# A three-pass fp32 decoder on one core: the fifth gate product in 512 columns

## The chip, the core and the metric

The kernel runs on one core of a Trainium2 chip. Its five engines work at the same time, each through its own queue in order: TensorE (PE; its weight loads are PEld), VectorE (DVE), ScalarE (ACT), GpSimd (POOL), and SyncE (SP), which issues DMAs. They wait for each other through semaphores. TensorE writes its results into PSUM banks of 128 x 512 floats; VectorE and ScalarE read them. The metric is the time of one execution in microseconds on the device, as the median of several runs.

## What is computed

A decoder of two layers over 512 tokens of width 1024: a gated short convolution in the first layer, sliding-window attention in the second, and behind each a SwiGLU feed-forward part. The change is in that part:

```python
def swiglu(h, w_gate_up, w_down):
    g, u = jnp.split(h @ w_gate_up, 2, axis=-1)
    return (jax.nn.silu(g) * u) @ w_down
...
    ff = swiglu(rmsnorm(h, ffn_pre_norm[l]), ffn_w_gate_up[l], ffn_w_down[l])
    h = h + rmsnorm(ff, ffn_post_norm[l])
```

`g` and `u` are 2816 wide, in 22 tiles of 128. All is float32.

## The kernel before

**Three passes.** A float32 operand `a` is split into `hi`, its value rounded to TensorE's fast format (`fp32r`), and `lo`, the rest `a - hi`. A product is `hi*lo + hi*hi + lo*hi`. `mm3` (L192 to L195) issues the three matmuls. ScalarE makes `hi` of the weights (L478), VectorE the rest `lo` (L479), on tiles of 128x1024.

**Seven products.** The first two tiles of gate and up are made plainly; the other 20 go in ten groups q0 to q9 per layer (`gate_jobs`). A group is a 2x2 block product, of two halves of the 1024 inputs, two halves of 256 tokens each, and of gate and up, and is computed with seven products instead of eight, from sums of the weight blocks and of the token halves. They run in the order 1, 2, 6, 5, 7, 3, 4. The sums of the token halves are made once per layer. The sums of the weight blocks come by accumulating DMAs that POOL issues (`Sums`, `issue`), for some groups (`ADDED`, q1 and q2 among them) partly by VectorE (L466).

**Banks.** Each product has two output tiles e = 0, 1 (gate and up) of 128 x 256 tokens. `chain` says into which bank a product goes. Products 1, 6, 7, 4 (chain X) accumulate in two banks `gx`, one for each e; in a bank, columns 0 to 255 belong to the rounded tokens and 256 to 511 to their rests: one matmul of 512 columns of `whi` does both (L1072), one of 256 columns of `wlo` with the rounded tokens follows (L1075), and the two column halves are added when they are read. Product 2 (Y, bank `gy`) and products 5 and 3 (Z, one bank `gz` for both e and both products) go through `mm3` in 256 columns. So a product is 16 matmuls in X, and 24 in Y and Z.

**Reading.** After each product `take` reads what has accumulated: `st` is the running sum of X without product 5, `u` the one with it. For products 1, 6 and 4 ScalarE copies the first column half of a bank to `st` and VectorE adds the second (L1050, L1034); for product 7 VectorE adds both halves to `u`. Product 5 alone is in `gz` when ScalarE copies it to `u` (L1039); product 3 is added on top of it in the bank, and VectorE adds the sum to `st` (L1034). A product of X may start only when the bank's state after the product before it has been read.

**Order.** Nothing reorders: each engine's instructions stand as the program issues them. `in_line` runs the products as a line of jobs. Behind job j it prepares the weights of job j + 3 (`LINE_LEAD`; a fetch by SP into one of `N_RAW` = 7 raw tiles, then L478 and L479), so that on VectorE the reading of a product stands ahead of the split for the third product after it. One step of the work left over from the group before (pair sums L593 and L594, splits L599 and L600) is put behind each job. After q2, q4, q6 and q9 come the seven products of the down projection for the groups finished by then (`px`, `py`, `pz`), whose sums VectorE adds up (L648).

Of the kernel before, what the change touches and what calls it, by code (L numbers as in the profile page):

```python
# [12 lines left out]
AF = mybir.ActivationFunctionType  # L13
# [61 lines left out]
def yoco_kernel(  # L75
# [22 lines left out]
    nc = tc.nc  # L98
# [9 lines left out]
    ps_mm = ctx.enter_context(tc.tile_pool(name="ps_mm", bufs=4, space=PSUM))  # L108
    ps_sc = ctx.enter_context(tc.tile_pool(name="ps_sc", bufs=2, space=PSUM))
    ps_pt = ctx.enter_context(tc.tile_pool(name="ps_pt", bufs=2, space=PSUM))  # L110
# [3 lines left out]
    def name(s):  # L114
        uid[0] += 1
        return f"{s}_{uid[0]}"

    def slot(s, dt=F32, w=S):
        return big.tile([P, w], dt, tag="slot", name=name(s), padded_shape=[P, S])

    def wide(s, dt=F32):
        return wides.tile([P, D], dt, tag="wide", name=name(s))
# [7 lines left out]
    def bank(s, pool=None):  # L130

        if pool is None:
            pool = (ps_mm, ps_sc, ps_mm, ps_pt)[turn[0] % 4]
            turn[0] += 1
        return pool.tile([P, S], F32, tag="bank", name=name(s))
# [56 lines left out]
    def mm3(out, whi, wlo, xhi, xlo, start, stop, **kw):  # L192
        nc.tensor.matmul(out, whi, xlo, start=start, stop=False, **kw)  # L193
        nc.tensor.matmul(out, whi, xhi, start=False, stop=False, **kw)  # L194
        nc.tensor.matmul(out, wlo, xhi, start=False, stop=stop, **kw)  # L195
# [256 lines left out]
    class Job:  # L452
# [10 lines left out]
        def add(self):  # L463
            if self.make:
                raw = self.raws[0].tile
                nc.vector.tensor_tensor(out=raw, in0=raw, in1=self.raws[1].tile, op=ALU.add)  # L466
# [90 lines left out]
    for l in range(2):  # L557
# [3 lines left out]
        for rd, (f0, f1) in enumerate(ROUNDS[:-1]):  # L561
            k = slice(f0 // 2, f1 // 2)
# [107 lines left out]
    with tc.manual_schedule(engines=ALL):  # L670
# [25 lines left out]
        for k in range(KT):  # L696
# [7 lines left out]
            for i in range(3):  # L704
                for t in range(3):
# [3 lines left out]
                                     start=k == i == 0, stop=k == KT - 1 and i == 2)  # L709
# [13 lines left out]
        v = small.tile([P, 4], F32, tag="v", name=name("v"))  # L723
# [100 lines left out]
    with tc.manual_schedule(engines=ALL):  # L824
# [21 lines left out]
        pools = {"p": ps_pt, "m": ps_mm, "s": ps_sc}  # L846
# [134 lines left out]
    def ffn(l, before, ahead, gain, gpres, following):  # L981
# [20 lines left out]
        def gate_jobs(q, factors, out, to, then):  # L1002

            sums = sums_of[f"g{l}{q}"]
            a21, a22, a11, a12 = (Raw(b) for b in sums.blocks)
            s1, s3, *rest = (Raw(b) for b in sums.sums)
            raws = {1: [a11], 2: [a12], 5: [s1], 7: [s3], 4: [a22]}
            if rest:  # L1010
                raws[6], raws[3] = ([r] for r in rest)
            else:
                raws[6], raws[3] = [a11, s1], [a12, a11]
            chain = {1: "X", 6: "X", 7: "X", 4: "X", 5: "Z", 3: "Z", 2: "Y"}
            pools = {"X": ps_mm, "Y": ps_pt, "Z": ps_sc}
            split = {}
            if q == 0:

                pools = {"X": ps_sc, "Y": ps_pt, "Z": ps_mm}
                raws[1], raws[2] = [], []  # L1020
                split = {1: ahead.ready[4], 2: ahead.ready[5]}
            banks, kept = {}, []

            def tiles(a):
                return a.rearrange("p (e c) -> p e c", e=2)

            def take(p):
                x, y, z = (banks.get(c) for c in "XYZ")
                st, u, gr = kept
                g0, g1 = (gr.rearrange("p (e h c) -> p e h c", e=2, h=2)[:, :, h]  # L1030
                          for h in range(2))

                def add(out, a, b):
                    nc.vector.tensor_tensor(out=out, in0=a, in1=b, op=ALU.add)  # L1034

                if p == 2:
                    add(g0, tiles(y), tiles(st))
                elif p == 5:
                    nc.scalar.activation(u, z, AF.Copy)  # L1039
                elif p == 3:  # L1040
                    add(g1, tiles(z), tiles(st))
                else:
                    for e in range(2):
                        a, b = x[e][:, :256], x[e][:, 256:]
                        ste, ue = (v[:, e * 256 : (e + 1) * 256] for v in (st, u))
                        if p == 7:
                            add(ue, a, ue)
                            add(ue, b, ue)
                            continue
                        nc.scalar.activation(ste, a, AF.Copy)  # L1050
                        add(ste, b, ste)
                if p == 4:
                    for g, m in ((g0, st), (g1, u)):
                        nc.vector.scalar_tensor_tensor(out=g, in0=tiles(m), scalar=-1.0, in1=g,
                                                       op0=ALU.mult, op1=ALU.mult)

            def run(p):
                def products(job):
                    if not kept:
                        kept.extend([slot("st"), slot("st"), wide("gr")])  # L1060
                    whi, wlo = split[p] if p in split else job.w
                    c = chain[p]
                    opened = c not in banks
                    if opened:
                        banks[c] = ([bank("gx", pools[c]) for _ in range(2)] if c == "X"
                                    else bank("g" + c.lower(), pools[c]))
                    steps = [(e, k, slice(e * S + k * P, e * S + (k + 1) * P))
                             for e in range(2) for k in range(4)]
                    kw = {"skip_group_check": True}
                    if c == "X":  # L1070
                        for e, k, kk in steps:
                            nc.tensor.matmul(banks[c][e], whi[:, kk], factors[p][k][2],  # L1072
                                             start=opened and k == 0, stop=False, **kw)
                        for e, k, kk in steps:
                            nc.tensor.matmul(banks[c][e][:, :256], wlo[:, kk], factors[p][k][0],  # L1075
                                             start=False, stop=k == 3 and p == 4, **kw)
                    else:
                        for e, k, kk in steps:
                            mm3(banks[c][:, e * 256 : (e + 1) * 256], whi[:, kk], wlo[:, kk],
                                *factors[p][k][:2], opened and e == k == 0,  # L1080
                                e == 1 and k == 3 and p in (2, 3), **kw)
                    take(p)
                return products

            def gate():
                nc.scalar.activation(kept[2], kept[2], AF.Silu)  # L1086

            def end():
                late = out(kept[2], to)
                then()  # L1090
                return late

            return [Job(raws[p], run(p), {3: gate, 4: end}.get(p), len(raws[p]) > 1)
                    for p in (1, 2, 6, 5, 7, 3, 4)]
# [42 lines left out]
        with tc.manual_schedule(engines=ALL):  # L1137
# [5 lines left out]
            def then(hf, k):  # L1143
                if hf == 0 and k in (5, 6):
                    for b in ((0, 1), (2, 3))[k - 5]:
                        before.turn(b, (2,))
                if hf == 0 and k == 6:
                    for b in range(4):
                        before.turn(b, (3,))
                    for f in range(KT):  # L1150
                        before.split(0, f, 1)
                    for b in range(4):
                        before.keep(b, 1)
                if hf == 1 and k == 1:
                    factors.update(before.factors())
                if hf == 1 and k == 3:
                    sum_on(f"{l}f0")
# [149 lines left out]
    class Heads:  # L1307
# [115 lines left out]
        def out(self):  # L1423
            if self.t < BOTH:
                hi, lo = halves("ohl", F32R)
            else:
                hi, lo = slot("ohi", F32R), slot("olo", F32R)
            nc.scalar.activation(hi, self.po, AF.Copy)
            nc.vector.tensor_tensor(out=lo, in0=self.po, in1=hi.bitcast(F32), op=ALU.subtract)
            at.append((hi, lo))  # L1430
# [25 lines left out]
    with tc.manual_schedule(engines=ALL):  # L1456
# [20 lines left out]
        for hf in range(2):  # L1477
            c = slice(hf * 256, (hf + 1) * 256)
# [54 lines left out]
    with tc.manual_schedule(engines=ALL):  # L1533
        sum_on("a0")
        for i in range(KT + 2):
# [9 lines left out]
            for c in order.split():  # L1545
# [11 lines left out]
                if op == "g":  # L1557

                    u = 2 * (t - EARLY - 1) + n[0]
# [126 lines left out]
```

## Time and profile before

| | |
|---|---|
| three runs | 1016.07, 1016.13, 1017.07 us, median 1016.13 |
| profiled execution, first to last instruction | 1014.9 us |
| TensorE busy, mean granted clock | 1007.0 us, 0.998 |
| VectorE, ScalarE, GpSimd busy | 867.8, 580.4, 193.8 us |
| gate groups of the first layer | q0 204.6 to 224.4, q1 to 244.2, q2 to 264.1; q3 to q9 between 292.7 and 469.6 |
| gate groups of the second layer | q0 from 702.2, q1 from 722.0, q2 741.8 to 761.7; q3 to q9 between 790.3 and 967.1 |

The profile gives the span of the profiled execution, and no other time of it; the runs were timed on the device from outside, with 1.2 us more. A matmul's row shows its start and a modelled end that overlaps the next one's; so how long a product takes is read from start to start. In a line of the timeline stand the start, the duration of all the merged instructions, the engine, the source line, the operation, out<-in, the shape and the count; in brackets the idle time before it and what ended it.

### The profile page before, as it was taken

How to read it: one execution, taken by the hardware profiler on the slowest of the kernel's cores; microseconds unless marked ns; L12 is line 12 of the kernel's file. 1: busy time of each engine (PE TensorE's matmuls, PEld its weight loads, DVE VectorE, ACT ScalarE, POOL GpSimd, SP SyncE). 2: the span in 40 equal slices, each digit the busy share in tenths (PEclk: the TensorE clock that was granted, in tenths of full speed). 3: DMA queues.
4: the chain of work that ended last, by engine and by line, in shares of the span. 5: the costliest groups of instructions: out<-in, count | busy, mean ns of one | idle time of the engine just before them, and what ended most of it. 6: DMA issues, size and time to landing. Idle time of an engine off the chain costs nothing.

```text
span 1014.9 us, 16253 instructions
## 1 busy us (share of the span) xinstructions
PE 1007.0 (99%) x6008; PEld 893.2 (88%) x6008; DVE 867.8 (86%) x1480; ACT 580.4 (57%) x1035; POOL 193.8 (19%) x259
## 2 busy tenths in 40 slices
PE   9999999999999999999999999999999999999997
PEld 8888888999889898998898888889998998989986
DVE  5766768899788999998878998779997899999896
ACT  6322544875656455566484786677666564645641
POOL 0443133102101011000032753221111010110001
PEclk9999999999999999999999999999999999999999
DMA  9897789549979789779603889976989676979842
GB/s 353 289 246 242 184 253 337 176 166 269 340 238 291 241 285 321 239 212 336 203 2 136 215 241 271 252 276 151 279 282 333 170 248 225 300 263 263 266 155 84
DMA packets 66576, 244.50 MB, mean 241 GB/s; under 512 B 7873, under 2 KB 8385, under 8 KB 54721
## 3 DMA queue, kind: packets, MB, share of 16 engines
q1 hardware_dynamic: 51328, 145.98, 38.8%
q0 software_dynamic: 14592, 96.48, 37.6%
q10 hardware_dynamic: 576, 1.02, 0.3%
q8 instruction: 47, 0.77, 0.3%
q14 instruction: 33, 0.26, 0.1%
HBM read 237.15 MB, written 102.76 MB: 335 GB/s over the span
## 4 chain that ended last, share of the span: by engine, by line
PE 99%; DVE 1%; issue 0%; DVEq 0%
PE gx L1072 15%; PE gx L1075 8%; PE gz L195 4%; PE gz L193 4%; PE gz L194 4%; PE pcub L193 4%; PE pcub L195 4%; PE pcub L194 4%; PE px L193 4%; PE px L194 4%; PE px L195 4%; PE pmix L193 3%; PE pmix L195 3%; PE pmix L194 3%; PE gy L195 2%; PE gy L194 2%
## 5 line engine op out<-in xcount | busy, mean ns | idle before, releaser
L479 DVE TENSOR_TENSOR wlo<-raw,whi 128x1024 fp32r<-128x1024 f32 x225 | 274.6, 1225 | 53.6 <-ACT whi L478 53.4
L478 ACT ACTIVATE whi<-raw 128x1024 fp32r<-128x1024 f32 x225 | 233.6, 1051 | 100.7 <-DVE raw L466 28.9
L1072 PE MATMUL gx<-xt,whi 128*128 128x512 f32 x480 | 120.4, 393 | 0.0
L1072 PEld LDWEIGHTS gx<-xt,whi 128*128 128x128 f32 x480 | 86.3, 189 | 15.5
L547 POOL DMA_DIRECT2D hsum<-in_w_gb_dram x96 | 62.8, 733 | 150.6 <-ACT whi L478 90.1
L547 POOL DMA_DIRECT2D hsum<-hsum x32 | 25.3, 790 | 295.5 <-ACT whi L478 198.2
L1034 DVE TENSOR_TENSOR st<-gx,st 128x256 f32<-128x256 f32 x200 | 78.0, 419 | 2.5 <-ACT st L1050 0.4
L1050 ACT ACTIVATE st<-gx 128x256 f32<-128x256 f32 x120 | 43.4, 380 | 62.6 <-PE gx L1075 58.9
L1075 PEld LDWEIGHTS gx<-xt,wlo 128*128 128x128 f32 x480 | 65.5, 190 | 4.7
L1075 PE MATMUL gx<-xt,wlo 128*128 128x256 f32 x480 | 66.9, 282 | 0.0
L1086 ACT ACTIVATE gr<-gr 128x1024 f32<-128x1024 f32 x20 | 21.2, 1062 | 49.9 <-DVE gr L1034 49.9
L193 PE MATMUL px<-wlo,ahi 128*128 128x512 f32 x120 | 46.7, 389 | 0.0
L194 PE MATMUL px<-whi,ahi 128*128 128x512 f32 x120 | 46.7, 389 | 0.0
L195 PE MATMUL px<-whi,alo 128*128 128x512 f32 x120 | 46.7, 389 | 0.0
L195 PE MATMUL gz<-xhi,wlo 128*128 128x256 f32 x160 | 45.5, 284 | 0.0
L193 PE MATMUL gy<-xlo,whi 128*128 128x256 f32 x160 | 45.3, 283 | 0.0
L194 PE MATMUL gy<-xhi,whi 128*128 128x256 f32 x160 | 45.3, 283 | 0.0
L195 PE MATMUL gy<-xhi,wlo 128*128 128x256 f32 x160 | 45.3, 283 | 0.0
L193 PE MATMUL gz<-xt,whi 128*128 128x256 f32 x160 | 45.3, 283 | 0.0
L194 PE MATMUL gz<-xt,whi 128*128 128x256 f32 x160 | 45.3, 283 | 0.0
L195 PE MATMUL gz<-xt,wlo 128*128 128x256 f32 x160 | 45.3, 283 | 0.0
L193 PE MATMUL gz<-xlo,whi 128*128 128x256 f32 x160 | 45.3, 283 | 0.0
(298 smaller groups left out, 2989.0 us busy)
## 6 DMA issues: line engine op xcount, KB each, us to landing
hsum<-in_w_gb_dram POOLq DMA_DIRECT2D x96, 512.0 KB, 7.8
raw<-hsum SPq DMA_DIRECT2D x88, 512.0 KB, 8.0
raw<-in_w_gb_dram SPq DMA_DIRECT2D x60, 512.0 KB, 7.0
hsum<-in_w_dn_dram POOLq DMA_DIRECT2D x36, 512.0 KB, 8.0
raw<-in_w_dn_dram SPq DMA_DIRECT2D x32, 512.0 KB, 6.3
hsum<-hsum POOLq DMA_DIRECT2D x28, 512.0 KB, 5.6
raw<-in_w_in_dram SPq DMA_DIRECT2D x21, 512.0 KB, 7.4
hsum<-in_w_dn_dram POOLq DMA_DIRECT2D x12, 768.0 KB, 12.9
```

The source lines that it names most:

```text
L193: nc.tensor.matmul(out, whi, xlo, start=start, stop=False, **kw)
L194: nc.tensor.matmul(out, whi, xhi, start=False, stop=False, **kw)
L195: nc.tensor.matmul(out, wlo, xhi, start=False, stop=stop, **kw)
L478: self.begun = nc.scalar.activation(hi[:, :n], raw, AF.Copy)
L479: nc.vector.tensor_tensor(out=lo[:, :n], in0=raw, in1=hi[:, :n].bitcast(F32), op=ALU.subtract)
L547: nc.gpsimd.dma_start(dst, src, max_dma_last_dim=4 * 4 * S, **kw))
L1034: nc.vector.tensor_tensor(out=out, in0=a, in1=b, op=ALU.add)
L1050: nc.scalar.activation(ste, a, AF.Copy)
L1072: nc.tensor.matmul(banks[c][e], whi[:, kk], factors[p][k][2], start=opened and k == 0, stop=False, **kw)
L1075: nc.tensor.matmul(banks[c][e][:, :256], wlo[:, kk], factors[p][k][0], start=False, stop=k == 3 and p == 4, **kw)
L1086: nc.scalar.activation(kept[2], kept[2], AF.Silu)
```

## The change

Product 5 takes the wide form of X: two banks (`gz`, one for each e), `whi` with 512 columns of rounded tokens and rests, `wlo` with 256 columns. Product 3 gets a bank of its own, `gv`, from the pool of product 2 (`ps_pt`), and stays in 256 columns. Since product 5 is no longer in product 3's bank, VectorE adds it to `st`; and since its two column halves are apart, ScalarE copies the first of each e to `u`, and VectorE adds the second.

```diff
-            chain = {1: "X", 6: "X", 7: "X", 4: "X", 5: "Z", 3: "Z", 2: "Y"}
-            pools = {"X": ps_mm, "Y": ps_pt, "Z": ps_sc}
+            chain = {1: "X", 6: "X", 7: "X", 4: "X", 5: "Z", 3: "V", 2: "Y"}
+            pools = {"X": ps_mm, "Y": ps_pt, "V": ps_pt, "Z": ps_sc}
             split = {}
             if q == 0:
 
-                pools = {"X": ps_sc, "Y": ps_pt, "Z": ps_mm}
+                pools = {"X": ps_sc, "Y": ps_pt, "V": ps_pt, "Z": ps_mm}
...
                 elif p == 5:
-                    nc.scalar.activation(u, z, AF.Copy)
+                    for e in range(2):
+                        ue = u[:, e * 256 : (e + 1) * 256]
+                        nc.scalar.activation(ue, z[e][:, :256], AF.Copy)
+                        add(ue, z[e][:, 256:], ue)
+                    add(st, u, st)
                 elif p == 3:
-                    add(g1, tiles(z), tiles(st))
+                    add(g1, tiles(v), tiles(st))
...
                     if opened:
-                        banks[c] = ([bank("gx", pools[c]) for _ in range(2)] if c == "X"
-                                    else bank("g" + c.lower(), pools[c]))
+                        banks[c] = ([bank("g" + c.lower(), pools[c]) for _ in range(2)]
+                                    if c in "XZ" else bank("g" + c.lower(), pools[c]))
...
-                    if c == "X":
+                    if c in "XZ":
                         for e, k, kk in steps:
                             nc.tensor.matmul(banks[c][e], whi[:, kk], factors[p][k][2],
                                              start=opened and k == 0, stop=False, **kw)
                         for e, k, kk in steps:
                             nc.tensor.matmul(banks[c][e][:, :256], wlo[:, kk], factors[p][k][0],
-                                             start=False, stop=k == 3 and p == 4, **kw)
+                                             start=False, stop=k == 3 and p in (4, 5), **kw)
```

VectorE in q1 of the first layer, from the sums of product 6 to those of product 7 (the number behind a name tells tiles apart; `raw`, `whi`, `wlo` are weights, `s`, `gr`, `ahi`, `alo` the left-over work of the group before). Before:

```order
L1034 TENSOR_TENSOR st_2238<-gx_2242,st_2238 128x256
L479 TENSOR_TENSOR wlo_2326<-raw_1994,whi_2325 128x1024
L593 TENSOR_TENSOR s_2236<-gr_2014 128x256
L594 SCALAR_TENSOR_TENSOR s_2236<-s_2235,gr_2014 128x256
L479 TENSOR_TENSOR wlo_2367<-raw_2076,whi_2366 128x1024
L600 TENSOR_TENSOR alo_2374<-s_2235,ahi_2373 128x512
L1034 TENSOR_TENSOR st_2239<-gx_2241,st_2239 128x256 x2
L1034 TENSOR_TENSOR st_2239<-gx_2242,st_2239 128x256 x2
```

The same place now:

```order
L1034 TENSOR_TENSOR st_2236<-gx_2240,st_2236 128x256
L479 TENSOR_TENSOR wlo_2324<-raw_1994,whi_2323 128x1024
L593 TENSOR_TENSOR s_2234<-gr_2014 128x256
L594 SCALAR_TENSOR_TENSOR s_2234<-s_2233,gr_2014 128x256
L1034 TENSOR_TENSOR st_2237<-gz_2338,st_2237 128x256
L1034 TENSOR_TENSOR st_2237<-gz_2339,st_2237 128x256
L1034 TENSOR_TENSOR st_2236<-st_2237,st_2236 128x512
L479 TENSOR_TENSOR wlo_2362<-raw_2076,whi_2361 128x1024
L600 TENSOR_TENSOR alo_2369<-s_2233,ahi_2368 128x512
L1034 TENSOR_TENSOR st_2237<-gx_2239,st_2237 128x256 x2
L1034 TENSOR_TENSOR st_2237<-gx_2240,st_2237 128x256 x2
```

Three adds stand between the pair sums and the next weight's rest; all else keeps its order.

ScalarE at the same place, around product 5. Before:

```order
L478 ACTIVATE whi_2325<-raw_1994 128x1024
L1039 ACTIVATE st_2239<-gz_2340 128x512
L478 ACTIVATE whi_2366<-raw_2076 128x1024
L599 ACTIVATE ahi_2373<-s_2235 128x512
L478 ACTIVATE whi_2397<-raw_2105 128x1024
```

The same place now:

```order
L478 ACTIVATE whi_2323<-raw_1994 128x1024
L1041 ACTIVATE st_2237<-gz_2338 128x256
L1041 ACTIVATE st_2237<-gz_2339 128x256
L478 ACTIVATE whi_2361<-raw_2076 128x1024
L599 ACTIVATE ahi_2368<-s_2233 128x512
L478 ACTIVATE whi_2392<-raw_2105 128x1024
```

One copy has become two of half the width; nothing else has moved.

More of the change, by code (lines that the diff above doesn't have):

```diff
@@ L1027, in take @@
             def take(p):
-                x, y, z = (banks.get(c) for c in "XYZ")
+                x, y, z, v = (banks.get(c) for c in "XYZV")
                 st, u, gr = kept
```

## The prediction

> **What bounds the kernel now.** I read the page first: its busy times, the granted clock and the chain that ended last.
>
> ```profile
> PE 1007.0 (99%) x6008; PEld 893.2 (88%) x6008; DVE 867.8 (86%) x1480; ACT 580.4 (57%) x1035; POOL 193.8 (19%) x259
> ...
> PEclk9999999999999999999999999999999999999999
> ...
> PE 99%; DVE 1%; issue 0%; DVEq 0%
> ```
>
> TensorE runs through almost without a gap at full clock and is 99% of the chain, so time taken out of its stream should come out of the total. But VectorE is at 86%, and that is a mean. So the second view was the busy time per stage: each row below is one gate group (seven products, q0, q1, q2, q5 of the first layer, then q1 and q2 of the second).
>
> ```profile
> core 0: us, PE busy (x) PEld busy (x) DVE busy (x) ACT busy (x) POOL busy (x), PEclk, DMA share, GB/s
> 204.61:224.42 19.81, 19.81 (x137) 18.47 (x137) 17.84 (x30) 14.24 (x22) 1.82 (x3) 1.00 0.63 213
> 224.42:244.25 19.83, 19.83 (x137) 18.47 (x137) 19.69 (x32) 12.37 (x20) 4.45 (x7) 1.00 0.72 202
> 244.25:264.15 19.90, 19.90 (x137) 18.52 (x137) 19.77 (x32) 12.38 (x20) 3.67 (x6) 1.00 1.01 328
> ...
> 351.24:371.03 19.79, 19.79 (x137) 18.47 (x136) 18.04 (x28) 11.65 (x17) 2.81 (x5) 1.00 0.71 252
> ```
>
> ```profile
> 721.98:741.79 19.81, 19.81 (x137) 18.47 (x137) 19.67 (x32) 12.35 (x19) 3.65 (x6) 1.00 0.89 295
> 741.79:761.70 19.91, 19.91 (x138) 18.52 (x137) 19.77 (x32) 12.38 (x20) 2.38 (x3) 1.00 0.85 245
> ```
>
> In q1 and q2 of either layer VectorE is busy 19.7 of 19.8 to 19.9 us: two engines are full there. In q5, as in the groups not shown, it has 1.3 to 3.4 us to spare. The chain of waits in order of time says the same: the eight wide matmuls of product 7, 1.84 us in nearly every group, take 0.1 us more in q2 of both layers.
>
> ```profile
> 255.59 1.94 PE gx L1072 x8
> ...
> 753.13 1.95 PE gx L1072 x8
> ```
>
> **The change, part by part.** *TensorE gains.* The timeline of TensorE in q5: product 6 (wide form), product 5 (old form, 24 matmuls of 256 columns), product 7 (wide form), and the start of product 3.
>
> ```profile
> 356.89 2.00 PE L1072 MATMUL gx<-xt,whi 128*128 128x512 f32 x8
> ...
> 359.68 0.28 PE L193 MATMUL gz<-xt,whi 128*128 128x256 f32 x1
> ...
> 362.56 2.00 PE L1072 MATMUL gx<-xt,whi 128*128 128x512 f32 x8
> ...
> 365.36 0.28 PE L193 MATMUL gz<-xlo,whi 128*128 128x256 f32 x1
> ```
>
> From start to start, the old form takes 362.56 - 359.68 = 2.88 us, the wide one 2.79 (359.68 - 356.89) and 2.80. The columns are the same, 6144; only eight starts fewer remain as a gain. Product 5 becomes 0.085 us shorter, 20 times: 1.7 us, which on a full TensorE all counts.
>
> The Trainium skill, TensorE: Matmul & The Clock Gate, section Back-to-back issue gap, puts the gap of matmuls at N/2.4 + 2.5 ns, which would make product 5 shorter by eight times 2.5 = 20 ns and the whole gain 0.4 us. The rows above say 0.085 us a product, and the measurement decides; by the page the sum below would be 0.9 us higher (0.065 less gain in seven groups of each layer).
>
> *ScalarE* copies product 5's first column half in two pieces of 128x256 instead of one of 128x512. The first bank is complete four matmuls before the second, so the first piece goes earlier. ScalarE is busy 12 to 14 of 19.8 us: nothing.
>
> *Banks.* Product 3 opens a bank in the pool of product 2; the two alternate, each read long before its next turn. Product 5's two banks are free again after VectorE's adds, one group ahead of their next use. Nothing, unless VectorE is a whole product behind.
>
> *VectorE* gets three adds behind product 5: two of 128x256 from the banks, one of 128x512 in SBUF. Nothing is taken from it. Its rows in q1 give the prices, and show the place: product 6's sums (235.03), a weight rest, two pair sums, then (at 237.50) the rest and the split before which the three adds now stand, and product 7's sums (239.23).
>
> ```profile
> 235.03 0.75 DVE L1034 TENSOR_TENSOR st<-gx,st 128x256 f32<-128x256 f32 x2
> 235.69 1.22 DVE L479 TENSOR_TENSOR wlo<-raw,whi 128x1024 fp32r<-128x1024 f32 x1
> ...
> 237.16 0.42 DVE L594 SCALAR_TENSOR_TENSOR s<-s,gr 128x256 f32<-128x256 f32 x1
> 237.50 1.22 DVE L479 TENSOR_TENSOR wlo<-raw,whi 128x1024 fp32r<-128x1024 f32 x1
> 238.63 0.69 DVE L600 TENSOR_TENSOR alo<-s,ahi 128x512 fp32r<-128x512 f32 x1
> 239.23 1.67 DVE L1034 TENSOR_TENSOR st<-gx,st 128x256 f32<-128x256 f32 x4
> ```
>
> ```profile
> 239.68 0.42 DVE L1034 TENSOR_TENSOR st<-gx,st 128x256 f32<-128x256 f32 x1
> ```
>
> What counts is from start to start, since instructions overlap a little. Two independent adds take 235.69 - 235.03 = 0.66, so 0.33 each. An add that needs the one before it starts 239.68 - 239.23 = 0.45 later. A 128x512 takes 239.23 - 238.63 = 0.60. So: first add 0.33, second 0.45 (the third reads its result), third 0.60: 1.38 us. Bounds: 0.33 + 0.33 + 0.60 = 1.26 if nothing waits, 0.42 + 0.42 + 0.69 = 1.53 if nothing overlaps. I take 1.38, as each of the three has its like in these rows.
>
> *Where the adds are hidden.* In q0, q5 and q6 VectorE sits idle at exactly this place, waiting for the next weight's rounding by ScalarE, which queues behind the copy of product 5:
>
> ```profile
> 216.01 0.42 DVE L594 SCALAR_TENSOR_TENSOR s<-s,gr 128x256 f32<-128x256 f32 x1
> 217.57 1.22 DVE L479 TENSOR_TENSOR wlo<-raw,whi 128x1024 fp32r<-128x1024 f32 x1 [1.14 <-ACT whi L478]
> ```
>
> ```profile
> 215.99 0.60 ACT L1039 ACTIVATE st<-gz 128x512 f32<-128x512 f32 x1 [1.55 <-PE gz L195]
> ```
>
> ```profile
> 364.34 1.23 DVE L479 TENSOR_TENSOR wlo<-raw,whi 128x1024 fp32r<-128x1024 f32 x1 [1.03 <-ACT whi L478]
> ...
> 384.15 1.22 DVE L479 TENSOR_TENSOR wlo<-raw,whi 128x1024 fp32r<-128x1024 f32 x1 [1.20 <-ACT whi L478]
> ```
>
> In q0 the adds can follow the pair sums at 216.35 (216.01 plus 0.34, as from 237.16 to 237.50) and end at 217.73, while the rest started at 217.57: 0.16 us late. The second bank's copy must end by 216.7 for that: it can begin where the old copy of both did, at 215.99, and take no longer, so it ends by 216.6. So q0 leaves a lag of 0.16, with 0 to 0.4 as bounds. The groups behind q2 have the same idle place, like q5 and q6 here; the 0.2 to 0.4 us that stick out of it meet the rest of their spare time (q5: 18.04 busy of 19.79). Eight groups of a layer pay nothing.
>
> *Where it is not.* From 217.57 until 270.3 VectorE has no gap beyond 0.04 us. A lag can't be made up there: it is 0.16 until product 5 of q1, 1.54 until product 5 of q2, 2.92 after it. TensorE feels it because products 6, 7 and 4 add into the banks that VectorE must have read after the product before: the next may start when the second half of the first bank is read. The three closest places, VectorE's last read and TensorE's start behind it (q2, before products 6, 7 and 4):
>
> ```profile
> 249.15 0.42 DVE L1034 TENSOR_TENSOR st<-gx,st 128x256 f32<-128x256 f32 x1
> ```
>
> ```profile
> 249.76 1.32 PE L1072 MATMUL gx<-xt,whi 128*128 128x512 f32 x5
> ```
>
> ```profile
> 254.95 0.42 DVE L1034 TENSOR_TENSOR st<-gx,st 128x256 f32<-128x256 f32 x1
> ```
>
> ```profile
> 255.43 0.73 PE L1072 MATMUL gx<-xt,whi 128*128 128x512 f32 x2
> ```
>
> ```profile
> 259.61 0.42 DVE L1034 TENSOR_TENSOR st<-gx,st 128x256 f32<-128x256 f32 x1
> ```
>
> ```profile
> 261.20 2.00 PE L1072 MATMUL gx<-xt,whi 128*128 128x512 f32 x8
> ```
>
> The middle pair is the wait already there: read until 255.37, start at 255.43, so the handover costs 0.06. With the lags: product 6 can start at 249.57 + 1.54 + 0.06 = 251.17 instead of 249.76 (1.41 late), product 7 at 255.37 + 1.54 + 0.06 = 256.97 (1.54 late), product 4 at 260.03 + 2.92 + 0.06 = 263.01 instead of 261.20 (1.81 late). These are not added: each is TensorE's delay so far, with its gain in q0 to q2 within it. Most of it falls in front of product 6 of q2.
>
> *What is late next.* After q2 come the down products, each of which needs its weight's rest. The tightest is the third:
>
> ```profile
> 266.80 3.49 DVE L479 TENSOR_TENSOR wlo<-raw,whi 128x1024 fp32r<-128x1024 f32 x3
> 273.96 3.50 DVE L479 TENSOR_TENSOR wlo<-raw,whi 128x1024 fp32r<-128x1024 f32 x3 [3.67 <-ACT whi L478]
> ```
>
> ```profile
> 269.46 0.39 PE L193 MATMUL px<-wlo,a 128*128 128x512 f32 x1
> ```
>
> It is ready at 266.80 + 1.22 = 268.02, with the lag at 270.94; it is wanted at 269.46 + 1.81 = 271.27. It holds by 0.33 us. Then 3.67 us of idle time take up VectorE's lag. The DMA issues of SP and POOL, paced by these splits, move by no more than that lag.
>
> *Sum.* A layer: +1.81 at the end of q2, minus 7 x 0.085 = 0.6 in q3 to q9: +1.21. The second layer has the same rows: +1.21. Together +2.4 us on a span of 1014.9. The median of the runs, 1016.13, lies 1.2 us above that span: 1016.1 + 2.4 = 1018.5. By the bounds (adds 1.26 to 1.53, q0's lag 0 to 0.4), a layer gives +0.8 to +1.75, and the time is 1017.7 to 1019.6.
>
> **Rivals.** *VectorE's adds are hidden everywhere, TensorE's gain alone remains*: 1016.1 - 1.7 = 1014.4, not slower. The place is product 4 of q2: TensorE starts 1.17 us after the read, less 0.06, so a lag under 1.11 costs nothing there; it decides whether three adds, paid twice, come to less than 0.5 us each time. For it speaks TensorE's 99%; against it the rows of 19.7 us. The Trainium skill, Perfetto Trace Analysis, section Identifying the Most-Contended Engine, calls the engine of highest occupancy the one to optimise first, which would be TensorE and this time; the same section grants that the engine can change over time, which the rows of q1 and q2 show. Chance 0.11.
>
> *The lag is paid once, not twice*: VectorE gains it back between product 5 of q1 and that of q2, as some of its waits shrink while TensorE stands. Then a layer costs 0.16 + 1.38 - 1.11 - 0.6 = -0.2, in all 1015.8. Against it: no gap is in those rows. Chance 0.15.
>
> *The lag spreads*: the down rests, held by 0.33 us, or weight tiles freed up to 2.9 us later, come too late; the DMA share of 1.01 in q2 leaves no room to catch up. Another 1 to 3 us a layer: 1020.5 to 1024.5. Chance 0.12.
>
> **How the numbers follow.** The forecast has 0.62, with 1017.7 to 1019.6 as its own range. A measurement tells about 0.2%, 2.0 us, from no change, so slower begins at 1018.2; the forecast reaches it unless the adds cost 1.28 or less: 0.50 of its 0.62 lie above. With the spreading lag, slower is 0.62. Same: 0.12 of the forecast, 0.15 of the lag paid once, 0.07 of the hidden adds, 0.34. Faster keeps 0.04, if the gain of 1.7 us is a little larger than it looks. The range 1015.6 to 1020.2 leaves out the hidden adds and most of the spreading lag, 0.2 together.
>
> **What would show it.** Product 5 from start to start 2.79 to 2.80 us. Behind it, three VectorE instructions at starts 0.33, 0.45 and 0.60 apart; in q0 and q5 VectorE's idle time there all but gone. In q1 and q2 VectorE without a gap for 21 us a group; product 6 of q2 about 1 us late in the chain of waits, product 4 of q2 about 1.8 us later than before, in both layers, and every other group 0.085 shorter. I am wrong if VectorE finds room in q1 or q2, if the adds cost less than 1.28, or if a down product of the first round waits for its weight.

## The result and the profile after

The changed kernel takes 1019.1 us (median of eight runs, 1018.79 to 1019.86) against 1016.42 before (eight runs, 1016.03 to 1017.07): a ratio of 1.0027, with a 95% interval of 1.0017 to 1.0037. It is 2.7 us slower. The profiled execution has a span of 1017.0 us (1014.9 before).

The page of the changed kernel: busy times, then the shares of the chain that ended last.

```profile
PE 1006.7 (99%) x5848; PEld 884.2 (87%) x5848; DVE 893.3 (88%) x1540; ACT 582.8 (57%) x1055; POOL 195.2 (19%) x259
...
PE 89%; DVE 8%; issue 2%; DMA 0%; DVEq 0%; SPq 0%; ACT 0%; ACTq 0%
```

TensorE issues 160 matmuls fewer, and VectorE is busy 25.5 us longer (867.8 to 893.3). The mean shares of the span hardly move. The chain does: VectorE held 1% of it, now 8%. That the end hangs on VectorE somewhere is read there, not in the 88%.

What TensorE's wide matmuls waited for, in the view of waits (us in total, times, longest us):

```profile
PE gx L1076 <- DVE st L1034: 2.2, 6, 0.7
```

Six waits in the whole run, three a layer (shorter ones are not listed). The busy times by stage say where: q0, q1, q2 of the first layer, then q1 and q2 of the second, in the columns of the same view of before.

```profile
203.62:223.35 19.73, 19.73 (x130) 18.05 (x129) 18.86 (x32) 14.17 (x23) 1.83 (x3) 1.00 0.63 213
223.35:243.88 20.53, 20.33 (x131) 18.21 (x129) 20.36 (x34) 11.74 (x20) 4.47 (x7) 1.00 0.72 205
243.88:264.90 21.02, 20.16 (x128) 17.92 (x127) 20.85 (x35) 12.32 (x20) 3.68 (x6) 1.00 0.95 316
...
722.38:742.89 20.51, 20.31 (x130) 18.22 (x129) 20.34 (x34) 11.74 (x20) 3.65 (x6) 1.00 0.85 287
742.89:764.20 21.31, 20.41 (x130) 18.18 (x129) 21.14 (x35) 12.34 (x20) 2.38 (x3) 1.00 0.85 250
```

Each row is length, then busy us by engine. q0 is 0.08 us shorter than before. q1 has grown by 0.7 us in either layer, and q2 of the second layer by 1.4. The row of q2 of the first layer ends 0.29 us before the group does (the first down product starts at 265.19), so q2 is 21.31 us long there and has grown by 1.4 too. VectorE is busy in all but 0.2 us of each row of q1 and q2: here it sets the pace, and TensorE now has idle time (20.16 busy of 21.02).

The timeline of TensorE in q5, from product 5 (now on `gz` in wide form) over product 7 to product 3:

```profile
360.71 2.00 PE L1076 MATMUL gz<-xt,whi 128*128 128x512 f32 x8
...
363.50 2.00 PE L1076 MATMUL gx<-xt,whi 128*128 128x512 f32 x8
366.30 0.28 PE L193 MATMUL gv<-xlo,whi 128*128 128x256 f32 x1
```

Product 5 takes 363.50 - 360.71 = 2.79 us from start to start (2.88 before), product 7 2.80 as before. The gain of the change is there, 0.09 us a product.

The timeline of VectorE in q0, from the second pair sum over the three adds (the first two in one row) to the next weight's rest:

```profile
215.20 0.42 DVE L594 SCALAR_TENSOR_TENSOR s<-s,gr 128x256 f32<-128x256 f32 x1
215.54 0.75 DVE L1034 TENSOR_TENSOR st<-gz,st 128x256 f32<-128x256 f32 x2
216.32 0.69 DVE L1034 TENSOR_TENSOR st<-st,st 128x512 f32<-128x512 f32 x1
216.93 1.22 DVE L479 TENSOR_TENSOR wlo<-raw,whi 128x1024 fp32r<-128x1024 f32 x1
```

The adds take 216.93 - 215.54 = 1.39 us. The bracket of idle time (1.14 us) in front of the rest is gone. In q1 the same rows stand at 236.85, 237.63 and 238.24: 1.39 again, with no idle time there to be used up.

Last, the places at which TensorE paid in q2: VectorE's read for which product 6 waits, and the start of product 6.

```profile
249.90 0.42 DVE L1034 TENSOR_TENSOR st<-gx,st 128x256 f32<-128x256 f32 x1
```

```profile
250.37 0.50 PE L1076 MATMUL gx<-xt,whi 128*128 128x512 f32 x1 [0.66 <-DVE st L1034]
```

And the same before product 4, where the read stood 1.2 us clear of TensorE before:

```profile
261.74 0.42 DVE L1034 TENSOR_TENSOR st<-gx,st 128x256 f32<-128x256 f32 x1
```

```profile
262.31 2.09 PE L1076 MATMUL gx<-xt,whi 128*128 128x512 f32 x8 [0.20 <-DVE st L1034]
```

From 217 us, the weight's rest in q0, until the second of these places the chain of waits of the changed kernel never comes to TensorE; it follows VectorE from instruction to instruction, and enters TensorE with product 4 of q2 (part of it):

```profile
248.84 1.14 DVE wlo L479
249.98 0.67 DVE st L1034 x2
...
261.74 0.44 DVE st L1034
262.18 0.14 issue
262.31 2.09 PE gx L1076 x8
```

**Where the 2.7 us came from.** The starts of TensorE's products can be taken from both traces and subtracted, product by product. From q0's start to the first down product, the changed kernel loses 2.02 us in either layer. Each product 5 in q3 to q9 then gives 0.09 back; in q9 product 6 costs 0.15 (it starts 0.04 late and takes 0.11 longer), and product 3 gives 0.11 back. In all 0.57 comes back a layer. So a layer costs 1.45 us, 2.9 in all. The spans differ by only 2.1, because in this execution the first matmuls of the program, far from the change, ran 0.8 us sooner; the medians, 2.7 apart, don't rest on one execution.

### The profile page after: what moved, and what is told of

Its sections match the earlier page's. It is cut to its first block, busy times and chain, and to the rows that moved or that the text cites. A ratio compares the mean times of both kernels' runs of the same rounds, so it can differ in the third digit from the quotient of the medians.

```text
span 1017.0 us, 16055 instructions
## 1 busy us (share of the span) xinstructions
PE 1006.7 (99%) x5848; PEld 884.2 (87%) x5848; DVE 893.3 (88%) x1540; ACT 582.8 (57%) x1055; POOL 195.2 (19%) x259
## 4 chain that ended last, share of the span: by engine, by line
PE 89%; DVE 8%; issue 2%; DMA 0%; DVEq 0%; SPq 0%; ACT 0%; ACTq 0%
PE gx L1076 12%; PE gx L1079 6%; PE pcub L194 4%; PE pcub L195 4%; PE pcub L193 4%; PE px L194 4%; PE px L193 4%; PE px L195 4%; PE gz L1076 3%; PE pmix L194 3%; PE pmix L193 3%; PE pmix L195 3%; DVE wlo L479 2%; PE pz L195 2%; PE pz L194 2%
## 5 line engine op out<-in xcount | busy, mean ns | idle before, releaser
L195 PE MATMUL gv<-xhi,wlo 128*128 128x256 f32 x160 | 45.3, 283 | 0.0
L193 PE MATMUL gv<-xlo,whi 128*128 128x256 f32 x160 | 45.3, 283 | 0.0
L194 PE MATMUL gv<-xhi,whi 128*128 128x256 f32 x160 | 45.2, 283 | 0.0
L547 POOL DMA_DIRECT2D hsum<-in_w_dn_dram x48 | 31.7, 754 | 46.5 <-ACT whi L478 31.3
L1076 PE MATMUL gz<-xt,whi 128*128 128x512 f32 x160 | 40.1, 392 | 0.0
```

Source lines behind the costliest of these rows:

```text
L547: nc.gpsimd.dma_start(dst, src, max_dma_last_dim=4 * 4 * S, **kw))
```

## The experiments

My theory, A: product 5's gain of 0.085 us is real in every group; the cost is VectorE's three adds, and only where VectorE has no idle time, in q1 and q2 of each layer. Each experiment was timed against the kernel before, run in turn on the same chip; its median there lay between 1016.5 and 1016.7. Differences below are between medians; the intervals are those of the ratio.

### Which groups pay

Two complements. The first keeps the old form in q1 and q2 alone, the second has the new form only there. Rival B says that the cost is spread over all groups.

```diff
+            apart = q not in (1, 2)      # second kernel: apart = q in (1, 2)
-            chain = {1: "X", 6: "X", 7: "X", 4: "X", 5: "Z", 3: "V", 2: "Y"}
+            chain = {1: "X", 6: "X", 7: "X", 4: "X", 5: "Z", 3: "V" if apart else "Z", 2: "Y"}
...
+                elif p == 5 and not apart:
+                    nc.scalar.activation(u, z, AF.Copy)
...
-                    add(g1, tiles(v), tiles(st))
+                    add(g1, tiles(v if apart else z), tiles(st))
...
-                    if c in "XZ":
+                    if c in ("XZ" if apart else "X"):
```

> The changed kernel with the old form of products 5 and 3 in q1 and q2 of both layers, the new one in the other sixteen groups. Theory A (VectorE is full in q1 and q2 alone, the adds cost only there, each group gains 0.085 us on TensorE): q0's lag of about 0.2 us still meets the tight places of q1 and q2 (+0.2 a layer), the seven groups behind gain 0.6, q9 gives 0.15 back: -0.3 a layer, about 0.6 us less than before. Theory B (adds or banks cost something in every group, 2.7 us over 20 groups): 16 of 20 shares, +2.1 us.

> The new form in q1 and q2 of both layers alone. Theory A: VectorE's lag 1.38 behind product 5 of q1, 2.76 behind that of q2; less the 1.17 of room in front of product 4 of q2, plus 0.1 to 0.2 for handover and restart: +1.7 to +1.8 a layer, about +3.5 us in all, more than the whole change costs. Theory B (a share in every group): 4 of 20, +0.5 us.

Without q1 and q2: 1015.66 us, 0.9 faster than before (0.998 to 0.9997). With them alone: 1020.38, 3.8 slower (1.0021 to 1.0045). The two add up to 2.9, near the change's cost (2.7 by the medians, 2.9 by the trace). In the trace of the second, each layer loses 1.84 us in q0 to q2, as A has it; B, which had +2.1 and +0.5, falls.

Sixteen products at 0.085 us would be 1.36; A took q0's lag off and had 0.6. From the start of its first gate group to the end of its last one the trace gains 0.76. It shows what is missing: 0.23 to 0.25 us a layer in q1, from q0's lag, and some 0.05 net in q9, as in the change.

### The two halves of the change apart

The adds alone: the kernel before, with three adds of the same shapes and kinds of operands put behind product 5's copy (what they write is overwritten later). And the new form alone: the changed kernel without the adds.

```diff
 # the adds alone, against the kernel before
                     nc.scalar.activation(u, z, AF.Copy)
+                    for e in range(2):
+                        c = slice(e * 256, (e + 1) * 256)
+                        add(gr[:, e * 512 + 256 : e * 512 + 512], y[:, c], u[:, c])
+                    add(g1, tiles(u), g1)
```

```diff
 # the new form alone, against the changed kernel
                         nc.scalar.activation(ue, z[e][:, :256], AF.Copy)
-                        add(ue, z[e][:, 256:], ue)
-                    add(st, u, st)
```

> The kernel before, with three VectorE adds of the same shapes behind product 5 that write a place overwritten later; the products and banks are the old ones. Theory A (VectorE's time is the whole cost): as the change without its gain on TensorE, and with 0.25 more lag from q0, where the old copy of both halves ends later: +2.2 to +2.5 a layer, +4.4 to +5.0 us. Theory C (the banks cost: product 3 in the pool of product 2, product 5 in both banks of its pool): no change, within 0.5 us of before.

> The changed kernel without the three VectorE adds behind product 5 (so the rests' half of product 5, and product 5 in the second sum, are left out of the result); products and banks are the new ones. Theory A: TensorE's gain alone, 20 x 0.085 = 1.7 us less than before, and up to 0.2 more where q2 waited 0.1 us. Theory C (the banks cost): +2.7 us, as with the whole change. Theory B: in between.

The new form alone: 1014.53 us, 2.06 faster (0.9968 to 0.9987). Its trace has no wait for VectorE on TensorE. This is the gain, at last undisturbed: 0.09 us off in each of the 20 groups, 1.7 in all, and 0.1 more in q9 of each layer, in product 3 (the next kernel shows why). The expectation looked for such an addition in q2; there it is 0.03.

The adds alone: 1022.55 us, 6.0 slower (1.0043 to 1.0068), a full microsecond above what A expected. The trace gives 2.3 us a layer in q1 and q2, as expected, and 0.86 a layer in q9, which A had as a group that pays nothing: 0.41 in product 6, by the lag that q8 hands on (the change has 0.15 there), and 0.45 in product 3. Theory C (the banks cost) falls with both kernels: the new banks alone cost nothing, the adds alone cost more than the change. For product 3, VectorE in q9, before:

```profile
462.63 1.22 DVE L479 TENSOR_TENSOR wlo<-raw,whi 128x1024 fp32r<-128x1024 f32 x1 [2.23 <-ACT whi L478]
```

And TensorE there, at the first matmul of product 3 that uses this rest:

```profile
463.91 0.39 PE L195 MATMUL gz<-xhi,wlo 128*128 128x256 f32 x1
464.13 0.28 PE L193 MATMUL gz<-xlo,whi 128*128 128x256 f32 x1
```

With the adds alone:

```profile
463.83 0.76 DVE L1034 TENSOR_TENSOR gr<-gy,st 128x256 f32<-128x256 f32 x2 [1.28 <-ACT st L1039]
464.62 0.69 DVE L1034 TENSOR_TENSOR gr<-st,gr 128x512 f32<-128x512 f32 x1
465.23 1.22 DVE L479 TENSOR_TENSOR wlo<-raw,whi 128x1024 fp32r<-128x1024 f32 x1
```

And TensorE there, in product 3:

```profile
465.91 0.28 PE L194 MATMUL gz<-xhi,whi 128*128 128x256 f32 x1
466.50 0.38 PE L195 MATMUL gz<-xhi,wlo 128*128 128x256 f32 x1 [0.31 <-DVE wlo L479]
```

VectorE had 2.23 us of idle time there, more than the adds need, but in this kernel it spends 1.28 of it waiting for ScalarE's copy of both halves, and the adds come behind that wait. The weight's rest behind them is wanted by product 3. In the kernel before it ended at 462.63 + 1.22 = 463.85, and TensorE used it at 463.91, 0.06 us later; the next matmul started 0.22 us behind, where 0.12 is usual. So there was no room at all. Idle time in front of an instruction is no cover if its result is wanted at once. In the changed kernel and in the new form alone ScalarE copies in two pieces and gets to this weight sooner; the wait does not appear, and the 0.1 us come back.

### How much of the adds must go

The changed kernel without the third add.

```diff
-                    add(st, u, st)
```

> The changed kernel without the third of the three adds (128x512); product 5 is left out of the second sum. Theory A (VectorE's lag in q1 and q2): two adds are 0.67 us a group. q0 hides them; behind product 5 of q1 the lag is 0.67, and products 6 and 7 of q2 had 0.13 and 0 us of room: +0.67 a layer at the end of q2. Behind q2's product 5 it is 1.34, within 0.3 us of what product 4 had, so nothing more. Then -0.6 in the seven groups behind, and q9 waits no more. Between -0.2 and +0.5 us against before, so between no adds (-2.1) and three (+2.7), not on the straight line between them (+1.1). Rival: the cost is proportional to the adds' time, +0.2 to +0.3 is a straight line through the origin at half the price; then q2's product 4 starts 0.9 us late a layer.

1015.6 us, 0.9 faster (0.9982 to 1.0: the interval touches no change): a miss of my expectation, which had it between -0.2 and +0.5. With no adds the time is 2.1 below before, with two 0.9 below, with three 2.7 above. So the first two cost 1.1 us and the third 3.6: not a price per add, but a delay that is free up to a point. What the expectation lacked is that q0 passes on not a lag of 0 but a lead of 0.3 us: with the copy in two pieces ScalarE gets to the next weight's rounding sooner, and VectorE to its rest (12.82 us after q0's start, 13.12 before). Two adds take 0.66 us in q2 (257.05 to 257.71); paid twice and less the lead, that is 1.0, and product 4 of q2 has 1.11 us of room. TensorE waits once in each layer, before product 6 of q2:

```profile
PE gx L1075 <- DVE st L1034: 0.5, 2, 0.3
```

### Less work for VectorE in q1 and q2

The weight sums that VectorE makes in q1 and q2 (L466) are left out in the first kernel, and made by accumulating DMAs, as in most other groups, in the second.

```diff
 # left out
-                raws[6], raws[3] = [a11, s1], [a12, a11]
+                raws[6], raws[3] = ([a11], [a12]) if q in (1, 2) else ([a11, s1], [a12, a11])
```

```diff
 # made by DMAs
-ADDED = (1, 2, 3, 4, 5, 7)
+ADDED = (3, 4, 5, 7)
```

> The changed kernel with VectorE's two sums of weight blocks left out in q1 and q2 (products 6 and 3 there use one block instead of a sum, so the result is another). Theory A: VectorE has 2 x 1.14 us more room in each of these groups, the three adds (1.4 us) fit in, and TensorE's gain remains: 1.4 to 1.9 us less than before. Rival (the three adds hold TensorE up by where they stand, not by VectorE's fullness): +2 us or more, as with the change.

> The changed kernel with all weight sums of q1 and q2 made by accumulating DMAs, as in q0, q6, q8 and q9, instead of two of them by VectorE. Theory A: VectorE gets the room as if they were left out, 1.4 to 1.9 us less than before, as long as the DMAs come in time. Rival E (the DMA engines are full there too, their share was 1.01 in q2 of the first layer): the weights come late, and it is slower than before by more than 1 us.

Left out: 1014.82 us, 1.9 faster (0.9978 to 0.9995; its runs scatter from 1014.1 to 1017.6). The profiled execution came 1.9 us late to q0 and had made that up by the end. With all three adds in place, TensorE waits nowhere in q1 and q2, and they are 0.1 and 0.2 us shorter than before; what was short there was VectorE's time, and not the place of the adds, as the rival had it.

Made by DMAs: 1030.74 us, 14 slower (1.0124 to 1.0152). A's gain had as its condition that the DMAs come in time; the rival, that they don't, is right, and by far more than it said. Busy time by stage, q2 of that kernel:

```profile
247.30:267.00 19.70, 19.70 (x129) 18.04 (x128) 18.17 (x32) 10.13 (x18) 3.66 (x6) 1.00 1.03 359
```

Its chain of waits, from q2 on (two long steps of many):

```profile
247.49 19.85 DMA raw<-hsum
...
273.52 15.73 DMA raw<-hsum
```

q2 is 19.70 us, not 21.31, and VectorE has 1.5 us to spare: the cure works where it is applied, and q1 and q2 gain as much as with the sums left out. But the DMA share in q2 is 1.03 (1.01 in the kernel before, 0.95 in the changed one), and a fetch of a summed block, in q2 and again behind it, is 16 to 20 us of the chain. The weights behind q2 come late, and TensorE loses 3.2 us in the first down round. It loses 8.6 more between the layers. There it waits for ScalarE's normalised tokens (4.0 us at once); the chain leads from them to GpSimd, whose own small steps of that normalisation stand in its queue behind the DMAs of the weight sums, 12 to 14 us each on the chain. The kernel also came 3.2 us late to q0; there it prepares the weights of the convolution in another order too, and that part is not explained here. In q2 there is nothing left on the DMAs to give.

### The adds on GpSimd

GpSimd is busy 19%. First the third add goes there; then all three (ScalarE copying both column halves).

```diff
-                    add(st, u, st)
+                    nc.gpsimd.tensor_tensor(out=st, in0=u, in1=st, op=ALU.add)
```

```diff
-                        add(ue, z[e][:, 256:], ue)
-                    add(st, u, st)
+                        ve = gr[:, e * S + 256 : (e + 1) * S]
+                        nc.scalar.activation(ve, z[e][:, 256:], AF.Copy)
+                        nc.gpsimd.tensor_tensor(out=ue, in0=ue, in1=ve, op=ALU.add)
+                    nc.gpsimd.tensor_tensor(out=st, in0=u, in1=st, op=ALU.add)
```

> The changed kernel with the third add behind product 5 (128x512, SBUF alone) on GpSimd instead of VectorE. Theory A (VectorE's lag): two adds are 0.67 us a group; q0 hides them, the lag is 0.67 behind product 5 of q1 and meets q2's products 6 and 7, which had 0.13 and 0 us of room: +0.7 a layer, then -0.6 by TensorE's gain: between 0 and +0.5 us against the kernel before, so about 2.3 us less than the whole change. Rival D (GpSimd's add of 1.3 us hinders VectorE or comes too late for product 3's sum): no better than the change, +2.7 us.

> The changed kernel with nothing of product 5 on VectorE: ScalarE copies both column halves, GpSimd adds them and adds the sum to the other one (128x512 about 1.3 us by its rows). Theory A: as with the adds left out, 1.5 to 2.0 us less than before, if GpSimd ends about 3 us behind product 5, when VectorE wants the sum for product 7. Rival D: GpSimd waits for the paced DMAs in its queue, or ScalarE's two more copies delay the weights: slower than before by 1 us or more.

One add moved: 1024.95 us, 8.3 slower (1.0071 to 1.0098). Three moved: 1034.33, 17.7 slower (1.0161 to 1.0189). Rival D, in the expectations, had the direction; neither loss was foreseen at that size. GpSimd's add in q0 and in q1, third add moved:

```profile
216.80 1.29 POOL L1043 TENSOR_TENSOR st<-st,st 128x512 f32<-128x512 f32 x1 [1.93 <-DVE st L1034]
...
238.71 2.21 POOL L1043 TENSOR_TENSOR st<-st,st 128x512 f32<-128x512 f32 x1 [2.09 <-DVE st L1034]
```

VectorE at the second of them:

```profile
238.54 1.21 DVE L479 TENSOR_TENSOR wlo<-raw,whi 128x1024 fp32r<-128x1024 f32 x1
239.68 1.79 DVE L600 TENSOR_TENSOR alo<-s,ahi 128x512 fp32r<-128x512 f32 x1
241.39 0.87 DVE L1034 TENSOR_TENSOR st<-gx,st 128x256 f32<-128x256 f32 x2
```

Read the three instructions by their ends. VectorE's rest runs from 238.54 at its usual 1.21 us. GpSimd's add starts at 238.71, inside it, and takes 2.21 instead of 1.29, until 240.92. VectorE's split takes 1.79 instead of 0.69, from 239.68 on: 1.1 us of standing still on the engine that has no time. In q0 it is the other way round: GpSimd starts first, at 216.80, and takes its 1.29; VectorE's rest, from 216.88, takes 2.30 instead of 1.22. The groups of that kernel say that it is no single case (mean ns behind the comma):

```profile
L600 DVE TENSOR_TENSOR alo<-s,ahi 128x512 fp32r<-128x512 f32 x40 | 38.4, 960 | 0.1
...
L1043 POOL TENSOR_TENSOR st<-st,st 128x512 f32<-128x512 f32 x20 | 36.0, 1802 | 55.7 <-DVE st L1034 55.7
```

The same splits before:

```profile
L600 DVE TENSOR_TENSOR alo<-s,ahi 128x512 fp32r<-128x512 f32 x40 | 27.4, 685 | 0.1
```

So the two engines don't run side by side here. The Trainium skill, SBUF — State Buffer, section SBUF: two separate sides, has the rule: VectorE and GpSimd share a pair of ports as an exclusive lock, which a VectorE instruction with two SBUF inputs takes against a GpSimd instruction that reads SBUF, and whoever starts first holds it for the whole instruction. The trace agrees: GpSimd gets through after the rest has ended (238.54 + 1.21 = 239.75, plus 1.29 is 241.04, against 240.92), and the split behind them ends 0.55 us after GpSimd. In the kernel with all three adds moved the splits take as long (959 ns), but ScalarE has two more copies there as well; how its 17.7 us divide was not tested.

### A version faster than both

The new form everywhere but in the groups that pay, or that hand a lag to one that pays: q0, q1, q2, and q8 ahead of q9.

```diff
+            apart = q not in (0, 1, 2, 8)
```

(The rest is as in the first experiment.)

> The new form in q3, q4, q5, q6, q7 and q9 of both layers, the old one in q0, q1, q2 and q8. Theory A: 12 x 0.085 = 1.0 us less than before, with no wait in q1, q2 and q9. It beats the form in all groups but q1 and q2 (-0.9) by too little to tell. Theory B (a share of the cost in every group): 12 of 20 shares, +1.6 us.

1015.5 us, 1.0 faster than before (0.9982 to 0.9999), with 12 products at 0.09 us, the 0.1 of q9 and no wait of TensorE for the adds: what A gives. It is 3.6 us below the change as it was made, by the medians, and, beside the first experiment's 0.9, the best of the versions that leave nothing out.

## Why the prediction was right

It said 1018.5, +2.4; measured were 1019.1, +2.7. Half of the difference of 0.6 is the kernel before, whose median over eight runs is 1016.42 instead of 1016.13. Step by step:

**TensorE's gain.** Forecast 0.085 us a product, found 0.09 in every group; the new form alone gains 2.06, a little more than 20 of these, because of q9. The formula that the prediction quotes from the Trainium skill, TensorE: Matmul & The Clock Gate, section Back-to-back issue gap, would have given 0.02. That section states it for an isolated matmul, and says that in a stream of weight loads and matmuls, as here, both set the spacing; so the runs show that it does not carry over to this stream, not that it is wrong.

**The price of the adds.** Forecast 1.38 us, found 1.39 in q0, q1 and q2. Reading prices from start to start in the trace of before was right.

**q0's lag.** Forecast 0.16, found 0.18 in the change. One part was not known: ScalarE's copy in two pieces was costed at nothing, and it lets VectorE's next rest start 0.3 us earlier, as the kernel with two adds shows. With three adds their own end comes later than that and decides, so the forecast did not suffer.

**Paid twice, in full groups.** Right, and shown by three experiments: nearly all cost lies in q1 and q2 when the groups are taken apart; it vanishes when VectorE's weight sums are left out there; and it grows by 3.6 us with the last add and 1.1 with the first two. Counted from q0's start, products 6, 7 and 4 of q2 start 1.43, 1.56 and 1.93 us late (forecast 1.41, 1.54, 1.81). The rival in which the lag is paid once falls, and so does the one in which the adds are hidden everywhere. (What the prediction quotes with the latter, that the most-contended engine can change over time, stands on the same page of the Trainium skill, Perfetto Trace Analysis, but in the next section, Optimization Strategy.)

**TensorE late by 1.81 at the end of q2.** Found 2.02 in either layer. The term mis-sized is the handover, put at 0.06. Before product 6 it is 250.37 less the read's end, 250.32: 0.05. Before product 4 it is 262.31 less 262.16, so 0.15, in q1 and q2 of both layers. Why is not shown; it is not the weight that ScalarE rounds for product 4, which was ready 4.7 us before (at 257.59). And eight wide matmuls behind a wait take 1.90 to 1.98 us rather than 1.84. The forecast left this out; only the restart of product 4 of q2 adds to the sum, the others go into the next wait. Nor did it fall where the forecast said, mostly in front of product 6 of q2: the prediction did not look at product 4 of q1, where VectorE's lag already exceeds the room. TensorE is 0.61 us late at the end of q1, and 0.8 more come before product 6 of q2. The sum is the same, since each is TensorE's delay so far.

**Eight groups pay nothing.** This step failed, if by little: in q9 product 6 pays 0.15 a layer, of which 0.11 comes back in product 3. VectorE's read of product 1's sums in q9, before and now:

```profile
454.55 0.75 DVE L1034 TENSOR_TENSOR st<-gx,st 128x256 f32<-128x256 f32 x2
```

```profile
455.43 0.75 DVE L1034 TENSOR_TENSOR st<-gx,st 128x256 f32<-128x256 f32 x2
```

Before, the first of the two was done at 454.97 (0.42 behind the start) and product 6 started at 455.18: 0.15 us of room, less the handover. Now the read stands 0.88 us later on a TensorE that reaches q9 0.68 later; this lag of 0.2 from q8 is more than the room. The forecast looked at q0, q5 and q6 and took the others to be like them.

**What is late next.** No down product waited for its rest, which had been forecast to hold by 0.33 us. The rival of a spreading lag falls for the change; the kernel with the sums by DMA is what it looks like.

With the two terms put right, the sum is 2 x (2.02 - 0.57) = +2.9 us by the traces; the medians say 2.7.

## What to carry to other kernels

Before work is moved to an engine that is 86% busy, read its busy time stage by stage, and when each of its results is wanted: here four groups of twenty had nothing left, and a gain of 2 us all over was outweighed by a loss of nearly 5, almost all in these four. An edit that pays in some stages and costs in others is worth making stage by stage, which turned +2.7 us into -1.0. Price the relief as carefully as the load: both ways tried to give its work to others (GpSimd, DMA) cost more than the burden.

## What the runs showed of the hardware

- An add on GpSimd holds up VectorE's instructions with two inputs from SBUF, and is held up by them: 1.79 us instead of 0.69 for a split of 128x512, 2.30 instead of 1.22 for a rest of 128x1024, 2.21 instead of 1.29 for the add. One add of 1.29 us per group moved to an engine that was 19% busy cost 8.3 us against the kernel before, where leaving it on VectorE cost 2.7.
- A matmul released by VectorE's read started 0.05 us after it before product 6, and 0.15 after it before product 4; behind a wait, eight wide matmuls took 1.90 to 1.98 us instead of 1.84. The cause of either is not settled by these runs.
- The first matmuls of the program differ from execution to execution of kernels that are equal up to there: the first three of 512 columns took 1.63 us in the profile of before and 1.03 in that of after; with the idle ones ahead of them, that moved all that followed by 0.8 us. Single profiles are compared from a stage's own start.
